# Depthwise convolution as 128x32 column blocks and a one-pass LayerNorm, in a hybrid trunk kernel

## The chip, the core and the metric

The kernel runs on one core of one Trainium2 chip. What counts is the device time of one execution in microseconds (us); the time before is the median of three runs. The profile shows one further execution, which was taken with the hardware profiler.

## The reference, cut to what matters

The program is a small diffusion backbone: four layers over 256 context and 256 latent tokens with 1024 channels, all in float32. Each layer has a token mixer and an MLP. The mixer of the second layer is a Conformer convolution, and that is where the change lies:

```python
def conformer_conv(h, w_pw1, b_pw1, w_dw, b_dw, ln_g, ln_b, w_pw2, b_pw2):
    z = h @ w_pw1 + b_pw1                      # h [B, L, 1024] -> [B, L, 2048]
    a, gt = jnp.split(z, 2, axis=-1)
    u = a * jax.nn.sigmoid(gt)
    u = lax.conv_general_dilated(u, w_dw[:, None, :], window_strides=(1,), padding=[(15, 15)],
                                 dimension_numbers=('NWC', 'WIO', 'NWC'), feature_group_count=1024) + b_dw
    u = jax.nn.silu(layer_norm(u, ln_g, ln_b))  # mean and variance over the 1024 channels of a token
    return u @ w_pw2 + b_pw2
```

The depthwise convolution gives each channel its own 31 taps along the tokens. It is run for the latent and for the context stream, separately padded.

## The kernel before, in words

All activations are kept transposed: a tile has 128 channels on the partitions and 512 tokens on the free axis (256 of the context, then 256 of the latent stream). Eight such tiles make up the 1024 channels. A float32 product is made from three matmuls at the single-pass rate: each operand is split into a high part and a rest (`hi`, `lo`), and `mm3` (L216) adds hi*hi, hi*lo and lo*hi. A weight unit of 128x1024 is loaded by a DMA into a buffer `raw` (six of them), ScalarE makes the high part `whi`, VectorE the rest `wlo` (L191; four buffers each). `project` (L222) runs the units one after the other and calls `done` on each finished PSUM bank. Dense matmuls use four PSUM banks; two banks (`w`) serve everything else in the mixer, and `nr` and `md` are single banks.

`conv(1)` (L796) has these steps. `glu(c)` (L800), for c from 0 to 7, projects the two units of channel tile c (48 matmuls of 128x512), takes the sigmoid on ScalarE and makes the tile `u` on VectorE. The depthwise convolution is shared out: tiles 0 to 2, and 3 and 4 stream by stream, are made on VectorE (`on_dve`, L826) by one multiply-add per tap; these steps stand in the list `todo`, and `taps_of` issues 12 of them per tile between the units. Tiles 5 to 7 are made on TensorE (`on_pe`, L862): for each tap GpSimd builds two 128x128 diagonal matrices (`affine_select`, L874, four taps at a time, two buffers), and three matmuls of 128x256 per tap and stream accumulate in PSUM (L882). The LayerNorm (`layer_norm`, L935) goes over one stream at a time, first the context, then the latent stream: sums over channels as matmuls with a column of ones (L943), the mean spread back over the partitions by matmuls (`spread`, L370), centring on VectorE (L957), squares on ScalarE, sums of squares, a root from Ln and Exp with a Newton step (`rsqrt`, L358), scaling (L972), SiLU and the high part on ScalarE, the rest on VectorE (L982). The second stream's tap work is woven into the first stream's LayerNorm (`norm_with`). Last, `out_project` (L432) multiplies by `conv_pw2`, adds the bias and the gated result to `x`, squares `x` for the next norm, and norms it for the MLP; its first four units run stream by stream, because of `apart`, and its last three do so too (`tail`).

The program is written with a scheduling layer that fixes the order of each engine's instructions when the kernel is built: what stands earlier in the program goes first, unless it isn't ready by the layer's own estimate of times. Semaphores and buffers follow from it. At run time each engine works through its list in order. The DMAs of weights are all issued from the SP queue, also in program order, and wait there for a free buffer.

Of the kernel before, what the change touches and what calls it, by code (L numbers as in the profile page):

```python
# [14 lines left out]
P = 128  # L15
# [28 lines left out]
PE_CONV = ((5, (0, 1)), (6, (0,)), (7, (0,)), (6, (1,)), (7, (1,)))  # L44
DVE_CONV = ((0, (0, 1)), (1, (0, 1)), (2, (0, 1)), (3, (0,)), (4, (0,)), (3, (1,)), (4, (1,)))
N_DG = 2
DG_TAPS = 4
LATE = 1
LATE_PE = 2
LN_LAG = 2  # L50
LN_ORDER = (0, 1, 2, 3, 4, 5, 6, 7)
DVE_TAPS = 12
# [22 lines left out]
CONV_ORDER = (0, 1, 2, 3, 4, 5, 6, 7)  # L75
# [3 lines left out]
def kernel(ctx: ExitStack, tc: tile.TileContext, io, out, depth=8):  # L79
# [716 lines left out]
    def conv(i):  # L796
        h = nxt.pop("h")
        cv = {}

        def glu(c):  # L800
            got = {}

            def done(n, p, zs):
                if n == 0:
                    got["a"] = p
                    taps_of(DVE_TAPS // 2)
                else:
                    sg = tmp("sg")
                    act(out=sg, in_=p, func=ACTF.Sigmoid, bias=par[:, C_BPW1 + 8 + c:C_BPW1 + 9 + c])
                    u = st("u")  # L810
                    stt(out=u, in0=got["a"], scalar=par[:, C_BPW1 + c:C_BPW1 + c + 1], in1=sg,
                        op0=ALU.add, op1=ALU.mult)
                    got["u"] = u
            project([io["conv_pw1"][c], io["conv_pw1"][8 + c]], h, (0, 1), done, first=2,
                    apart=c == CONV_ORDER[0])
            return got["u"]

        taps = [PAD] + [w for w in range(TAPS) if w != PAD]
        us = {}
# [4 lines left out]
        row = []  # L824

        def on_dve(c, zs):  # L826

            def step(n, w):
# [3 lines left out]
                if n == 0:  # L832
                    if c not in cv:
                        cv[c] = st("cv")
                    ins = ts(out=cv[c][:, span(zs)], in0=us[c][:, span(zs)], scalar1=tap, scalar2=bias_of(c),
                             op0=ALU.mult, op1=ALU.add).ins
                    if zs == (1,):
                        for name in row:
                            behind(ins, name, "the first stream first")
                else:  # L840
                    a3, u3 = [t.rearrange("p (z t) -> p z t", z=2)[:, zs[0]:zs[-1] + 1] for t in (cv[c], us[c])]
                    ins = stt(out=a3[:, :, lo:hi], in0=u3[:, :, lo + s:hi + s], scalar=tap, in1=a3[:, :, lo:hi],  # L842
                              op0=ALU.mult, op1=ALU.add).ins
                    if n == TAPS - 1 and zs != (1,):
                        row.append(ins.name)
# [15 lines left out]

        def on_pe(c, zs):  # L862

            got = {}

            def step(n, w):
                if n == 0:
                    got["u"] = ready.pop((c, zs), None) or split(c, zs)
                    got["ps"] = bank("cvps", "w")
                if n % DG_TAPS == 0:  # L870
                    k = min(DG_TAPS, TAPS - n)
                    got["dg"] = sm.tile([P, 2 * DG_TAPS, P], FR, tag="dg", name="dg", bufs=N_DG)
                    m = (pe_tiles.index(c) * TAPS + n) * 2
                    nc.gpsimd.affine_select(  # L874
                        out=got["dg"][:, 0:2 * k],
                        in_=tap_flat[:, m:m + 2 * k].unsqueeze(2).to_broadcast([P, 2 * k, P]),
                        pattern=[[0, 2 * k], [1, P]], compare_op=ALU.is_equal, fill=0.0, base=0,
                        channel_multiplier=-1)
                dg = [got["dg"][:, 2 * (n % DG_TAPS) + q] for q in range(2)]
                for q, part in ((0, 0), (0, 1), (1, 0)):  # L880
                    for z in zs:
                        mm(out=got["ps"][:, half(z)], lhsT=dg[q], rhs=got["u"][z][part][:, w:w + N_CTX],  # L882
                           start=n == 0 and q == part == 0 and z == zs[0], stop=n == TAPS - 1 and q == 1 and z == zs[-1])
                if n == TAPS - 1:
                    if c not in cv:
                        cv[c] = st("cv")
                    act(out=cv[c][:, span(zs)], in_=got["ps"][:, span(zs)], func=ACTF.Identity, bias=bias_of(c))
            return [lambda n=n, w=w: step(n, w) for n, w in enumerate(taps)]


        pe_tiles = sorted({c for c, _ in PE_CONV})
        tap_flat = cst.tile([P, len(pe_tiles) * TAPS * 2], F32, name="tap_hl")
        tap_hl = tap_flat.rearrange("p (c w q) -> p c w q", w=TAPS, q=2)
        t_ = par[:, C_TAP:C_TAP + KD * TAPS].rearrange("p (c w) -> p c w", c=KD)
        t_ = t_[:, pe_tiles[0]:pe_tiles[-1] + 1]
        for o, w in enumerate((slice(PAD, PAD + 1), slice(0, PAD), slice(PAD + 1, TAPS))):
            o = (slice(0, 1), slice(1, PAD + 1), slice(PAD + 1, TAPS))[o]
            act(out=tap_hl.bitcast(FR)[:, :, o, 0], in_=t_[:, :, w], func=ACTF.Copy)
            tt(out=tap_hl.bitcast(FR)[:, :, o, 1], in0=t_[:, :, w], in1=tap_hl[:, :, o, 0], op=ALU.subtract)
# [13 lines left out]
        ready = {}  # L913
        for n, c in enumerate(CONV_ORDER):
            us[c] = glu(c)
            for c_, zs in PE_CONV:
                if c_ == c:
                    ready[c, zs] = split(c, zs)
            for c_, zs in DVE_CONV:
                if c_ == c and zs != (1,):  # L920
                    merge(todo, on_dve(c, zs))
            if n:
# [3 lines left out]
        def both(a, b):
            while a or b:
                for q in (a, b):
                    if q:
                        q.pop(0)()  # L930

        both(todo, pe_todo)
        y = [(htile("yhi", FR), htile("ylo", FR)) for _ in range(KD)]

        def layer_norm(z):  # L935

            c_ = half(z)
            blocks = (2 * z, 2 * z + 1)
            got = {}

            def add(name, t, c):
                for n, b in enumerate(blocks):
# [448 lines left out]
```

## Time and profile before

| | us |
|---|---|
| median of three runs | 2227.54 (2226.61 to 2229.44) |
| profiled execution | 2229.72 |
| its span, first to last instruction | 2228.0 |
| TensorE busy | 2171.2 (97%) |
| VectorE busy | 1636.3 (73%) |
| ScalarE busy | 868.8 (39%) |
| GpSimd busy | 58.2 (3%) |
[...]

The profiled execution's own time is 1.7 us more than its span. Busy shares are averages over the whole program; the stage of the convolution is some 250 us of it, and its shares are read from windows of the trace. A matmul's busy time overlaps with the next one's, so the pace of matmuls is read from the distance between starts.

### The profile page before, as it was taken

Reading aid. Unit: us, or ns where it says so; the run is one execution under the profiler, and the core shown is the slowest. Engines: PE = TensorE matmul, PEld = TensorE weight load, DVE = VectorE, ACT = ScalarE, POOL = GpSimd, SP = SyncE. Lnnn points to the kernel's source line nnn. Section 1 sums busy time; section 2 is a strip of 40 time slices with the busy share of each in tenths; the row PEclk is TensorE's granted clock in tenths of the full one; section 3 lists DMA queues with packets and bytes.
Section 4 is the critical chain, followed back from the end, with each engine's and each line's share of the span. In section 5 each row is a group of like instructions: output and inputs, shape, how many; then the busy total and the mean of one; then the engine's idle time right before and its main releaser. Section 6 shows DMA issues by size and latency. Waiting matters only on the chain.

```text
span 2228.0 us, 33427 instructions
## 1 busy us (share of the span) xinstructions
PE 2171.2 (97%) x13162; PEld 1856.8 (83%) x13162; DVE 1636.3 (73%) x2989; ACT 868.8 (39%) x1495; POOL 58.2 (3%) x68
## 2 busy tenths in 40 slices
PE   6999999999999979999999998999999999999999
PEld 5777898888888979988888887788888889889999
DVE  4565577788859985777888579857788776687665
ACT  4443343233233205532322367734232324554443
POOL 0000000000000251000000000000000000000000
PEclk9999999999999979999999999999999999999999
DMA  8543334555522110345555311014455542234553
GB/s 304 173 149 133 113 103 148 184 173 198 188 98 93 39 38 10 105 149 192 170 198 181 104 67 64 14 63 146 152 192 188 177 170 86 85 114 132 186 182 117
DMA packets 83965, 299.57 MB, mean 134 GB/s; under 512 B 9440, under 2 KB 10976, under 8 KB 83808
## 3 DMA queue, kind: packets, MB, share of 16 engines
q1 hardware_dynamic: 83808, 297.44, 39.1%
q8 instruction: 103, 1.69, 0.3%
q14 instruction: 54, 0.44, 0.1%
HBM read 296.35 MB, written 1.05 MB: 133 GB/s over the span
## 4 chain that ended last, share of the span: by engine, by line
PE 88%; DVE 8%; ACT 1%; issue 1%; POOL 0%; DMA 0%; SPq 0%; POOLq 0%; DVEq 0%; ACTq 0%
PE ps L218 22%; PE ps L219 21%; PE ps L220 21%; DVE cv L842 4%; PE one L218 2%; PE one L219 2%; PE one L220 2%; PE ps L275 2%; PE ps L277 2%; PE ps L276 2%; PE o L719 1%; DVE wlo L197 1%; PE modps L292 1%; PE cvps L882 1%; PE sums L383 1%; PE sps L667 1%
## 5 line engine op out<-in xcount | busy, mean ns | idle before, releaser
L110 ACT ACTIVATE whi<-raw 128x1024 fp32r<-128x1024 f32 x366 | 387.1, 1059 | 883.2 <-PE ps L219 621.5
L197 DVE TENSOR_TENSOR wlo<-raw,whi 128x1024 fp32r<-128x1024 f32 x366 | 445.3, 1226 | 162.1 <-ACT whi L110 160.9
L218 PE MATMUL ps<-hi,whi 128*128 128x512 f32 (+1 forms) x1336 | 463.6, 348 | 0.0
L219 PE MATMUL ps<-lo,whi 128*128 128x512 f32 (+1 forms) x1336 | 461.1, 345 | 0.0
L220 PE MATMUL ps<-hi,wlo 128*128 128x512 f32 (+1 forms) x1336 | 460.9, 345 | 0.0
L218 PE MATMUL ps<-hhi,whi 128*128 128x512 f32 (+1 forms) x1240 | 437.5, 355 | 3.3 <-ACT hhi L110 3.3
L219 PE MATMUL ps<-hlo,whi 128*128 128x512 f32 (+1 forms) x1240 | 437.9, 354 | 0.0
L220 PE MATMUL ps<-hhi,wlo 128*128 128x512 f32 (+1 forms) x1240 | 436.4, 353 | 0.0
L308 DVE SCALAR_TENSOR_TENSOR macc<-modraw,cs,macc 128x512 f32<-128x512 f32 x504 | 346.9, 745 | 0.0
L218 PEld LDWEIGHTS ps<-hi,whi 128*128 128x128 f32 x1336 | 252.7, 189 | 34.0 <-issue 3.6
L220 PEld LDWEIGHTS ps<-hi,wlo 128*128 128x128 f32 x1336 | 253.0, 189 | 30.4
L219 PEld LDWEIGHTS ps<-lo,whi 128*128 128x128 f32 x1336 | 253.1, 189 | 30.1 <-issue 0.3
L218 PEld LDWEIGHTS ps<-hhi,whi 128*128 128x128 f32 x1240 | 234.3, 190 | 38.5 <-ACT hhi L110 4.0
L220 PEld LDWEIGHTS ps<-hhi,wlo 128*128 128x128 f32 x1240 | 235.1, 190 | 31.4
L219 PEld LDWEIGHTS ps<-hlo,whi 128*128 128x128 f32 x1240 | 235.4, 190 | 31.1
L449 DVE SCALAR_TENSOR_TENSOR x<-ps,mod,x 128x256 f32<-128x256 f32 x264 | 118.7, 480 | 173.6 <-PE ps L220 172.2
L842 DVE SCALAR_TENSOR_TENSOR cv<-u,par,cv 128x498 f32<-128x498 f32 (+28 forms) x210 | 128.0, 679 | 0.4
L110 ACT ACTIVATE hi<-sq 128x512 fp32r<-128x512 f32 (+1 forms) x128 | 73.7, 576 | 104.5 <-DVE sq L464 104.5
L204 DVE TENSOR_TENSOR lo<-sq,hi 128x512 fp32r<-128x512 f32 (+1 forms) x128 | 79.4, 620 | 22.1 <-ACT hi L110 22.1
L218 PE MATMUL one<-hhi,whi 128*128 128x512 f32 (+1 forms) x256 | 95.1, 372 | 0.3 <-DVE r L589 0.3
L219 PE MATMUL one<-hlo,whi 128*128 128x512 f32 (+1 forms) x256 | 91.5, 357 | 0.0
L220 PE MATMUL one<-hhi,wlo 128*128 128x512 f32 (+1 forms) x256 | 91.0, 355 | 0.0
(217 smaller groups left out, 2785.3 us busy)
## 6 DMA issues: line engine op xcount, KB each, us to landing
modraw<-in_w_mod SPq DMA_DIRECT2D x192, 512.0 KB, 3.8
raw<-in_w_mlp_in SPq DMA_DIRECT2D x128, 512.0 KB, 4.0
raw<-in_w_mlp_out SPq DMA_DIRECT2D x128, 512.0 KB, 3.3
raw<-in_conv_pw SPq DMA_DIRECT2D x24, 512.0 KB, 3.3
raw<-in_gla_v SPq DMA_DIRECT2D x16, 512.0 KB, 4.1
raw<-in_gla_r SPq DMA_DIRECT2D x16, 512.0 KB, 3.8
raw<-in_gla_out SPq DMA_DIRECT2D x16, 512.0 KB, 3.7
raw<-in_attn_qkv SPq DMA_DIRECT2D x12, 512.0 KB, 3.2
```

What stands on the lines that cost most here:

```text
L110: ins = nc.scalar.activation(**kw).ins
L197: tt(out=lo, in0=raw, in1=hi.bitcast(F32), op=ALU.subtract)
L204: tt(out=lo[:, cols], in0=src, in1=hi.bitcast(F32)[:, cols], op=ALU.subtract)
L218: mm(out=o, lhsT=wh[:, wsl], rhs=ah[:, cols], start=first, stop=False)
L219: mm(out=o, lhsT=wh[:, wsl], rhs=al[:, cols], start=False, stop=False)
L220: mm(out=o, lhsT=wl[:, wsl], rhs=ah[:, cols], start=False, stop=last)
L275: mm(out=ps[t], lhsT=ah[:, tok], rhs=wh[:, sl], start=kk == order[0] and i == 0, stop=False)
L276: mm(out=ps[t], lhsT=al[:, tok], rhs=wh[:, sl], start=False, stop=False)
L277: mm(out=ps[t], lhsT=ah[:, tok], rhs=wl[:, sl], start=False, stop=kk == order[-1] and i == 1)
L308: stt(out=acc, in0=raw[:, h], scalar=c, in1=acc, op0=ALU.mult, op1=ALU.add)
L449: stt(out=x[:, m, c], in0=src[:, c], scalar=gate[:, m, z:z + 1], in1=x[:, m, c], op0=ALU.mult, op1=ALU.add)
L842: ins = stt(out=a3[:, :, lo:hi], in0=u3[:, :, lo + s:hi + s], scalar=tap, in1=a3[:, :, lo:hi], op0=ALU.mult, op1=ALU.add).ins
```

## The change

The convolution on TensorE takes over tiles 3 to 7, and VectorE keeps tiles 0 to 2 for both streams at once. GpSimd's diagonal matrices, the split of `u`, and the work stream by stream go. Instead:

- `regroup` copies the tile `u` with sixteen VectorE copies of 32 partitions x 128 tokens into `ut`: 32 channels x 4 token phases on the partitions, and on the free axis four groups of 128 (two streams of 64 groups of four tokens).
- `on_pe` works with 34 tap matrices per tile (`BLOCKS`: shift m by groups of four tokens, output phase q). Each is a 128x128 block of which 32 columns belong to each channel group g. They are made on the host and loaded by DMA from the new array `conv_tz`, eight to a transfer of 512 KB into a `raw` buffer (five transfers per tile, the last of 128 KB). For each block and each g one float32 matmul with 32 columns and 2 x (64-|m|) tokens writes 32 partitions of the bank, every fourth token.
- `on_pe(c)` stands one tile behind `glu`: that of tile 3 after `glu(4)`, of tile 6 after `glu(7)`, and that of tile 7 inside the LayerNorm.
- 16 instead of 12 taps per tile are issued between the units.
- The LayerNorm goes over both streams at once. An early mean, from tiles 0 to 5, is taken off before the squares are made; the sums over the centred tiles and their squares give the rest of the mean and the variance; the root is a power of -0.5 on GpSimd.
- `out_project` runs its first four units together over both streams, without `apart`.

```diff
-PE_CONV = ((5, (0, 1)), (6, (0,)), (7, (0,)), (6, (1,)), (7, (1,)))
-DVE_CONV = ((0, (0, 1)), (1, (0, 1)), (2, (0, 1)), (3, (0,)), (4, (0,)), (3, (1,)), (4, (1,)))
...
-DVE_TAPS = 12
+PE_CONV = (3, 4, 5, 6, 7)
+PH = 4
+
+BLOCKS = tuple((m, q) for m in (0, -4, -3, -2, -1, 1, 2, 3, 4) for q in range(PH)
+               if any(0 <= PH * m + p - q + PAD < TAPS for p in range(PH)))
+TZ = 1024 // P
+DVE_TAPS = 16
...
+                    u = us[c] = st("u")
...
+            project([io["conv_pw1"][c], io["conv_pw1"][8 + c]], h, (0, 1), done, first=2, apart=c == 0)
...
+
+
+        def regroup(c):
+
+            ut[c] = st("ut")
+            u = us[c].rearrange("p (x j) -> p j x", j=PH)
+            for g in range(4):
+                for j in range(PH):
+                    nc.vector.tensor_copy(out=ut[c][32 * j:32 * j + 32, P * g:P * g + P],
+                                          in_=u[32 * g:32 * g + 32, j])
+
+        def on_pe(c):
+            ps = bank("cvps", "w")
+            o4 = ps.rearrange("p (z s j) -> p j z s", z=2, j=PH)
+            u4 = ut[c].rearrange("p (g z s) -> p g z s", g=4, z=2)
+            for n, (m, q) in enumerate(BLOCKS):
+                if n % TZ == 0:
+                    tz = wp.tile([P, 1024], F32, tag="raw", name="tz", bufs=N_BUF["raw"])
+                    w = P * min(TZ, len(BLOCKS) - n)
+                    nc.sync.dma_start(out=tz[:, 0:w], in_=io["conv_tz"][PE_CONV.index(c), n // TZ, :, 0:w])
+                lo, hi = max(0, -m), min(P // 2, P // 2 - m)
+                for g in range(4):
+                    r = slice(32 * g, 32 * g + 32)
+                    o = n % TZ * P + 32 * g
+                    mm(out=o4[r, q, :, lo:hi], lhsT=tz[:, o:o + 32], rhs=u4[:, g, :, lo + m:hi + m],
+                       start=n == 0, stop=n == len(BLOCKS) - 1)
+            cv[c] = st("cv")
+            act(out=cv[c], in_=ps, func=ACTF.Identity, bias=bias_of(c))
...
+        waiting = []
+        for c in range(KD):
+            glu(c)
+            if c in PE_CONV:
+                regroup(c)
+                waiting.append(c)
+                if len(waiting) > 1:
+                    on_pe(waiting.pop(0))
+            else:
+                merge(todo, on_dve(c))
+            if c:
                 taps_of(DVE_TAPS - DVE_TAPS // 2)
+        taps_of(len(todo))
+        load_table("silu_and_others")
...
+
+        blocks = (0, 1, 2, 3)
+        early = range(KD - 2)
+
+        def total(ps, t, first, last):
+            for n, b in enumerate(blocks):
+                mm(out=ps[:, n:n + 1], lhsT=t[:, b * P:b * P + P], rhs=ones, start=first and n == 0,
+                   stop=last and n == 3)
+
+        def column(name):
+            return sm.tile([P, 4], F32, tag="ln_" + name, name="ln_" + name, bufs=1)
+
+        acc = st("acc")
+        tt(out=acc, in0=cv[0], in1=cv[1], op=ALU.add)
+        for c in early[2:]:
+            tt(out=acc, in0=acc, in1=cv[c], op=ALU.add)
+        ps = bank("sums", "md")
+        total(ps, acc, True, True)
+        k_col = column("k")
+        ts(out=k_col, in0=ps[:, 0:4], scalar1=1.0 / (P * len(early)), scalar2=None, op0=ALU.mult)
+        k_row = spread(k_col, blocks)
+        sq = {}
+
+        def centre(c):
+            tt(out=cv[c], in0=cv[c], in1=k_row, op=ALU.subtract)
+            sq[c] = st("lnsq")
+            act(out=sq[c], in_=cv[c], func=ACTF.Square)
+
+        for c in early:
+            centre(c)
+        s2 = bank("lnsq", "w")
+        on_pe(waiting.pop(0))
+        for c in early:
+            total(s2, sq[c], c == 0, False)
+        s1 = bank("sums", "md")
+        for c in (KD - 2, KD - 1):
+            centre(c)
+            total(s1, cv[c], c == KD - 2, c == KD - 1)
+            total(s2, sq[c], False, c == KD - 1)
+        m, v, q, power = column("m"), column("v"), column("q"), column("power")
+        nc.vector.memset(power, -0.5)
+        ts(out=m, in0=s1[:, 0:4], scalar1=1.0 / D, scalar2=None, op0=ALU.mult)
+        m_row = spread(m, blocks, "nr")
+        tt(out=q, in0=m, in1=m, op=ALU.mult)
+        ts(out=v, in0=s2[:, 0:4], scalar1=1.0 / D, scalar2=EPS, op0=ALU.mult, op1=ALU.add)
+        tt(out=v, in0=v, in1=q, op=ALU.subtract)
+        nc.gpsimd.tensor_tensor(out=v, in0=v, in1=power, op=ALU.pow)
+        r_row = spread(v, blocks, "w")
...
+        for c in range(KD):
+            tt(out=cv[c], in0=cv[c], in1=m_row, op=ALU.subtract)
+            tt(out=cv[c], in0=cv[c], in1=r_row, op=ALU.mult)
+            act(out=cv[c], in_=cv[c], func=ACTF.Silu, scale=par[:, C_LNG + c:C_LNG + c + 1],
+                bias=par[:, C_LNB + c:C_LNB + c + 1])
+            act(out=y[c][0], in_=cv[c], func=ACTF.Copy)
+            tt(out=y[c][1], in0=cv[c], in1=y[c][0].bitcast(F32), op=ALU.subtract)
         load_table(EXP_LN)
         out_project(2 * i, [io["conv_pw2"][m] for m in range(8)], y, (0, 1), modt[i][:, 16:24],
-                    bias=par[:, C_BPW2:C_BPW2 + 8], extra=1, apart=True)
+                    bias=par[:, C_BPW2:C_BPW2 + 8], first=4)
...
+    w, r = f["conv_w_dw"][0].reshape(TAPS, KD, 4, 32), np.arange(32)
+    tz = np.zeros((len(PE_CONV), len(BLOCKS), PH, 32, 4, 32), np.float32)
+    for n, c in enumerate(PE_CONV):
+        for b, (m, q) in enumerate(BLOCKS):
+            for p in range(PH):
+                t = PH * m + p - q + PAD
+                if 0 <= t < TAPS:
+                    tz[n, b, p, r, :, r] = w[t, c].T
+    tz = tz.reshape(len(PE_CONV), len(BLOCKS), P, P)
+    tz = np.concatenate([tz, np.zeros((len(PE_CONV), -tz.shape[1] % TZ, P, P), np.float32)], axis=1)
+    a["conv_tz"] = tz.reshape(len(PE_CONV), -1, TZ, P, P).transpose(0, 1, 3, 2, 4).reshape(len(PE_CONV), -1, P, 1024)
```

## Rows read from the trace of the kernel before

**Rows 1.** Windows: stretch, its us, then busy us (instructions) per engine, clock, DMA share, GB/s.

```profile
680.40:754.20 73.80, 73.80 (x330) 61.19 (x329) 73.48 (x130) 18.47 (x25) 0.00 (x0) 1.00 0.25 86
754.20:809.20 55.00, 45.59 (x374) 44.90 (x372) 54.93 (x58) 5.10 (x8) 30.14 (x24) 0.95 0.11 33
809.20:858.10 48.90, 42.31 (x283) 41.71 (x283) 36.39 (x91) 13.57 (x30) 23.83 (x14) 0.78 0.02 8
858.10:913.40 55.30, 55.30 (x417) 54.08 (x418) 29.53 (x69) 30.58 (x58) 0.00 (x0) 0.94 0.14 48
```

**Rows 2.** Chain of work that ended last, 754 to 862 us: shares, then start, us, what.

```profile
by line: DVE cv L842 44.3%; PE cvps L882 23.1%; POOL dg L874 9.9%; PE sums L943 8.9%; DVE wlo L197 4.7%; PE lnsq L943 2.8%; issue 1.2%; PE ps L218 1.2%; PE rows L374 1.0%; PE ps L219 0.8%; PE ps L220 0.8%; DVE ulo L859 0.6%; DVE u L811 0.6%
...
757.68 40.48 DVE cv L842 x39
...
809.25 5.28 PE sums L943 x24
```

**Rows 3.** Timeline of TensorE: start, us, line, operation, tiles, shape, count.

```profile
749.65 0.39 PE L218 MATMUL ps<-hhi,whi 128*128 128x512 f32 x1
...
753.50 0.39 PE L220 MATMUL ps<-hhi,wlo 128*128 128x512 f32 x1
...
858.06 0.56 PE L218 MATMUL ps<-yhi,whi 128*128 128x256 f32 x1
...
907.75 0.28 PE L218 MATMUL ps<-yhi,whi 128*128 128x256 f32 x1
...
913.39 0.28 PE L220 MATMUL ps<-yhi,wlo 128*128 128x256 f32 x1
```

**Rows 4.** Timeline of TensorE around matmuls of 32 columns (two records each).

```profile
40.70 3.66 PE L292 MATMUL modps<-modraw,cs 128*32 128x256 f32 x64
...
661.99 0.28 PE L220 MATMUL ps<-hi,wlo 128*128 128x256 f32 x1
662.20 0.66 PE L314 MATMUL modps<-macc,pick 128*32 128x128 f32 x16
662.79 0.39 PE L218 MATMUL ps<-hhi,whi 128*128 128x256 f32 x1
```

**Rows 5.** Chain of work over the span: full-width float32 matmuls, two records each.

```profile
247.32 2.88 PE o L719 x24
...
666.40 0.79 PE sums L383 x8
```

**Rows 6.** Timeline of VectorE, 680 to 800 us.

```profile
680.41 0.74 DVE L811 SCALAR_TENSOR_TENSOR u<-ps,par,sg 128x512 f32<-128x512 f32 x1
...
682.78 6.85 DVE L842 SCALAR_TENSOR_TENSOR cv<-u,par,cv 128x482 f32<-128x482 f32 x9
...
697.45 3.33 DVE L842 SCALAR_TENSOR_TENSOR cv<-u,par,cv 128x488 f32<-128x488 f32 x5
...
734.85 1.23 DVE L197 TENSOR_TENSOR wlo<-raw,whi 128x1024 fp32r<-128x1024 f32 x1
...
774.18 23.98 DVE L842 SCALAR_TENSOR_TENSOR cv<-u,par,cv 128x492 f32<-128x492 f32 x18
```

**Rows 7.** Instructions of lines 156 and 1178: duration ns min/median/max, starts, forms.

```profile
L156 DVE CAST ident_r<-ident x1: 227/227/227, 4.3 to 4.3; 128x128 fp32r<-128x128 f32 x1
...
L1178 DVE CAST k<-kT x3: 282/283/284, 1317.2 to 1328.3; 128x128 fp32r<-128x128 f32 x3
```

**Rows 8.** Groups by line, 846 to 880 us: count, busy us, mean ns, idle before.

```profile
L972 DVE TENSOR_TENSOR cv<-cv,rows 128x256 f32<-128x256 f32 x16 | 5.7, 414 | 3.0 <-PE rows L374 3.0
...
L110 ACT ACTIVATE cv<-cv,par 128x256 f32<-128x256 f32 x16 | 9.0, 590 | 5.4 <-DVE cv L972 5.4
...
L110 ACT ACTIVATE yhi<-cv 128x256 fp32r<-128x256 f32 x16 | 6.1, 404 | 0.0
```

**Rows 9.** Groups by line of GpSimd, whole span.

```profile
L874 POOL TENSOR_SCALAR_AFFINE_SELECT dg<-tap_hl 128x768 fp32r<-128x768 f32 x5 | 5.0, 993 | 2.8 <-PE cvps L882 2.8
L856 POOL MEMSET ulo<- 128x15 f32 x12 | 0.9, 111 | 43.3 <-PE ps L219 43.2
```

**Rows 10.** The page: GB/s in 40 slices; a DMA issue with count, KB, us to landing.

```profile
GB/s 304 173 149 133 113 103 148 184 173 198 188 98 93 39 38 10 105 149 192 170 198 181 104 67 64 14 63 146 152 192 188 177 170 86 85 114 132 186 182 117
...
raw<-in_conv_pw SPq DMA_DIRECT2D x24, 512.0 KB, 3.3
```

More of the change, by code (lines that the diff above doesn't have):

```diff
@@ L832, in step @@
                 if n == 0:
[L833 to L839, printed above, removed]
-                else:
[L841 to L845, printed above, removed]
@@ L862, in on_pe @@
[L862 to L888, printed above, removed]
@@ L891, in conv @@
[L891 to L899, printed above, removed]
+                    cv[c] = st("cv")
@@ L911, in taps_of @@
             del todo[:n]
[L913 to L922, printed above, removed]
-                taps_of(DVE_TAPS - DVE_TAPS // 2)
-        pe_todo = [f for c, zs in PE_CONV if zs != (1,) for f in on_pe(c, zs)]
@@ L926, in both @@
[L926 to L932, printed above, removed]
-        y = [(htile("yhi", FR), htile("ylo", FR)) for _ in range(KD)]
[L935 to L942, printed above, removed]
-                    mm(out=got[name][:, n:n + 1], lhsT=t[:, b * P:b * P + P], rhs=ones,
-                       start=c == 0 and n == 0, stop=c == KD - 1 and n == 1)
-            def total(c):
-                if c == 0:
-                    got["sum"] = bank("sums", "w")
-                add("sum", cv[LN_ORDER[c]], c)
-            def mean():
-                m = sm.tile([P, 2], F32, tag="ln_m", name="ln_m", bufs=2)
-                ts(out=m, in0=got["sum"][:, 0:2], scalar1=1.0 / D, scalar2=None, op0=ALU.mult)
-                got["mean"] = spread(m, blocks)
-            def centre(c):
-                tt(out=cv[c][:, c_], in0=cv[c][:, c_], in1=got["mean"][:, c_], op=ALU.subtract)
-            def square_(c):
-                got[c] = tmp("lnsq")
-                act(out=got[c][:, c_], in_=cv[c][:, c_], func=ACTF.Square)
-            def total_sq(c):
-                if c == 0:
-                    got["sq"] = bank("lnsq", "w")
-                add("sq", got[c], c)
-            def root():
-                got["r"] = spread(rsqrt(got["sq"][:, 0:2], 2, 1.0 / D), blocks, "md")
-            def scale(c):
-                tt(out=cv[c][:, c_], in0=cv[c][:, c_], in1=got["r"][:, c_], op=ALU.mult)
-            def silu(c):
-                act(out=cv[c][:, c_], in_=cv[c][:, c_], func=ACTF.Silu, scale=par[:, C_LNG + c:C_LNG + c + 1],
-                    bias=par[:, C_LNB + c:C_LNB + c + 1])
-            def high(c):
-                act(out=y[c][0][:, c_], in_=cv[c][:, c_], func=ACTF.Copy)
-            def low(c):
-                tt(out=y[c][1][:, c_], in0=cv[c][:, c_], in1=y[c][0].bitcast(F32)[:, c_], op=ALU.subtract)
-            def staged(*stages):
-                steps = [[] for _ in range(KD + sum(l for l, _ in stages))]
-                o = 0
-                for lag, f in stages:
-                    o += lag
-                    for c in range(KD):
-                        steps[o + c].insert(0, (f, c))
-                return [lambda fs=fs: [f(c) for f, c in fs] for fs in steps]
-            return ([lambda c=c: total(c) for c in range(KD)] + [mean]
-                    + staged((0, centre), (1, square_), (LN_LAG, total_sq)) + [root]
-                    + staged((0, scale), (1, silu), (1, high), (1, low)))
```

50 lines of the change are left out of this document (7 added, 43 removed).

## The prediction

> **What bounds the kernel now.** I read the page first (TensorE 97% busy, so the program is a TensorE program), then the busy time of every engine in windows of the convolution stage, then the chain of waits there, then the timelines of TensorE and VectorE, and last the groups of instructions for prices. In the windows the reader is to see four stretches [rows 1]. From 680 to 754 us the `conv_pw1` projections keep TensorE full at the full clock; VectorE is as full (73.5 of 73.8 us). From 754 to 809 VectorE alone is full and TensorE has holes. From 809 to 858 the granted clock averages 0.78 and VectorE has holes too: the first stream's LayerNorm with the second stream's taps. From 858 to 913 TensorE is full with `conv_pw2`, at a mean clock of 0.94. The chain of waits [rows 2] says who ends last between 754 and 862: VectorE's taps (44%), then the tap matmuls (23%), and GpSimd's diagonals (10%). The taps there are slow ones: 18 of them take 23.98 us, 1.33 each, while GpSimd works for 30 of the 55 us; before GpSimd starts, five take 3.33, 0.67 each [rows 1, 6].
>
> So the stage stands as follows on TensorE [rows 3]. A 128x512 matmul starts every 0.2265 us ((753.50-749.65)/17), a 128x256 one every 0.12 ((913.39-907.75)/47). The projections end at 753.7, the first `conv_pw2` matmul starts at 858.1, the last ends its turn at 913.5. Between lie 104.4 us for convolution and LayerNorm, and 55.4 for `conv_pw2`. The prediction is where these two points, 858.1 and 913.5, come to lie. What follows 913.5 is the same program, so it is shifted whole.
>
> **The column blocks.** Removed are 558 matmuls of 128x256 (93 per tile and stream, for tiles 5 to 7): 67 us at 0.12, the GpSimd diagonals and the wait on them. Added are 34 blocks x 4 = 136 float32 matmuls for each of five tiles, with 32 columns and on the mean 124 tokens. Two lines of the kernel before are of this form [rows 4], two records per matmul: 64 records with 256 tokens in 3.66 us, 0.057 each, and 16 records with 128 tokens in 0.66, of which the last one's own 0.28 overlaps nothing, so 0.025 each. A full-width float32 matmul of 128 tokens takes 0.12 a record [rows 5]; so the four column groups do run beside each other. The bounds for a matmul here are 0.05 (two records at 0.025) and 0.114 (as slow as 256 tokens); with the full-width row as the far end, 0.24. I take 0.053, by the row that has the same number of tokens: 7.2 us a tile, against 15.5 and 32.6. A visit to this form costs at its two ends: the block of 16 starts 0.09 later than the matmul before would have let it, and the next starts 0.17 after its sixteen turns are over (662.79-662.62), 0.26 together. One visit per tile costs 0.3 us, one per transfer 1.3, one per block 8.8; with one per tile I take 7.5 us a tile.
>
> [...]
>
> **The loads.** Per tile come 2.2 MB of matrices, with the two weight units 3.2 MB for each step of 10.9 + 7.5 us: 175 GB/s. One slice of before moved 304, and this stretch 86, so they lie hidden [rows 1, 10]. They share the six `raw` buffers and the SP queue with the weight units, so a weight unit of the next tile queues behind a matrix that waits for its buffer. At 3.3 us from issue to landing, seven transfers strictly one after another would take 23 us instead of 18.4; that is priced with the first rival.
>
> **VectorE.** From 680.4, the first `u`, up to the last `u` it has: 11 `wlo` at 1.23 (13.5), 7 `u` at 0.74 (5.2), 93 taps, of which 12 in tile 0's own chain at 0.76 and 81 interleaved at 0.67 (63.4), and 64 regrouping copies [rows 6]. No row has a copy of 32 partitions with tokens four apart. The nearest, a 128x128 copy, is 0.227, one from PSUM 0.283 [rows 7]; below, 0.14, if each begins 0.09 before the last one ends, as the step of 0.67 within taps of 0.76 suggests. I take 0.227: 14.5. The sum is 96.6, so VectorE is free for the last `u` at 777.0. TensorE is through `glu(7)` at 753.7 + 3 x 7.5 = 776.2. That is a tie, and the order decides: in the steps of tiles 2, 3 and 4, before any column blocks, VectorE needs 16 x 0.67 + 2 x 1.23 + 0.74 = 13.9 us (17.5 with a regrouping) against TensorE's 10.9. That adds up to 12.6 us, and the four `wlo` buffers, which run one tile ahead, cover a part. The wait added is `u` and `wlo` behind taps in VectorE's list; TensorE waits for both. I take 8 us lost, between 0 and 16 (12.6 and one more regrouping, 3.6). `glu(7)` ends at 784.2, call it A.
>
> [...]
>
> **LayerNorm.** Column blocks of tiles 6 and 7 follow A: 15.0 us, and 0.9 for the second's bank, which the first must leave. The early sums, the early mean, and centring and squaring of six tiles (six of 0.74 on VectorE, of 0.62 on ScalarE) lie beside tile 7's blocks; if that cover is gone, they cost about 6. Then 24 sums of squares at 0.2 (0.79/4), 4.8, and 16 more for the last two tiles, 3.2 [rows 5]: A + 23.9. Then the tail: three small vector steps at 0.2, the power on GpSimd, which no row has (0.11 to 0.99, I take 0.5) [rows 9], four float32 matmuls of `spread` at 0.24, scaling 0.7, SiLU on 512 tokens about 0.8 (0.59 for 256), high part 0.6 [rows 8]: 4.2 us. The first `conv_pw2` matmul starts at A + 28.1 = 812.3, where before had 858.1.
>
> **`conv_pw2`.** Five units of 24 at 0.2265 and three by halves, 48 at 0.12: 44.5 us instead of 55.4, since no norm of a second stream lies among them. VectorE delivers a tile every 2.1 us (three steps of 0.7), the four units use 12 x 0.2265 = 2.7 for it, so TensorE sets the pace. I add 2 us for the clock, which at 858 was low after a thinly filled stretch (a first matmul of 0.56 instead of 0.28) [rows 3], and 2 for the buffers at the change from four units to one. It ends at 860.8 instead of 913.5: 52.7 us earlier.
>
> **The sum.** From the profiled execution's 2229.72 us (span 2228.0, 1.7 around it) that leaves 2177.0. It was 2.2 above the median of the runs, so I predict 2175.
>
> **Rivals.** First, the column blocks go at the pace of the 256-token row, 15.5 us a tile, because issue or the loads hold them: 5 x 8.0 more, less the 8 of lost order, which VectorE then no longer costs: +32, 2207. For it: the only long run of such matmuls is that row; against it: the short one is twice as fast. [...] Second, VectorE becomes the bound: copies at 0.283 (80 x 0.056 = 4.5) and 16 us of order lost instead of 8: +12.5, 2188. For it: VectorE is full already [rows 1]; against it: its slow taps go with GpSimd's work. Third, slower than before: with matrices and tokens that change at every matmul the column groups don't run beside each other, 0.24 a matmul, 32.6 us a tile: 5 x 25.1 - 8 = +117, 2292. It decides from 0.144 us a matmul, where 5 x (19.6 - 7.5) eats 52.7 + 8. Against it stand both rows of 32 columns. Fourth, the order costs nothing and the clock stays up: 2165 or a little less.
>
> **Chances.** Forecast 0.58, first rival 0.17, second 0.12, third 0.06, fourth 0.07. The range of 2156 to 2212 leaves out the third, the slower end of the first and the far end of the fourth, about 0.15. About 0.2% is what a measurement can tell from no change here. Faster by more: 0.89; within it, 0.03 (column blocks near 0.144); slower, 0.08.
>
> **What would show it.** Right: column-block records at 0.025 to 0.03, 35 to 38 us of TensorE for five tiles; taps at 0.67 throughout, GpSimd all but idle; copies at 0.23; first `conv_pw2` matmul 125 to 140 us after the first `u`, and about 48 us from there to the MLP. Wrong: records at 0.055 or more; TensorE waiting for `conv_tz` transfers; holes in TensorE ahead of a `wlo` or `u`; over 32 us from the end of `glu(7)` to `conv_pw2`; a low clock all through the LayerNorm.

## The result and the profile after

The changed kernel takes 2196.81 us (median of four runs, 2194.72 to 2199.41) against 2228.41 for the kernel before in the same session (2226.61 to 2229.44): a ratio of 0.986, 95% interval 0.9843 to 0.9877. That is 31.6 us faster. The forecast was 2175, inside a range of 2156 to 2212: the direction came as said and the column blocks cost what was forecast, but of the 53 us forecast some 21 are missing. The profiled execution took 2197.8 us (span 2196.0), and against this one the account is made. In the later sessions, in which the changed kernel was not run again, the kernel before took about 2251 us in a part of its executions and 2227 to 2231 in the others, so the experiments are read by their own medians, against the changed kernel's 2196.8, and a difference of a few us between sessions shows little.

The page's busy times, to be read beside the table of before: of GpSimd's 58.2 us 1.2 are left, VectorE lost 45, TensorE 29.

```profile
PE 2142.3 (98%) x13836; PEld 1816.5 (83%) x13836; DVE 1591.6 (72%) x2921; ACT 858.4 (39%) x1455; POOL 1.2 (0%) x5
```

The windows of the stage, with the columns of [rows 1]: projections with the blocks of tiles 3 to 5 (three rows), last column blocks, LayerNorm, `conv_pw2`.

```profile
683.00:713.00 30.00, 30.00 (x133) 24.50 (x132) 29.68 (x44) 5.28 (x7) 0.00 (x0) 1.00 0.22 71
713.00:745.00 32.00, 24.65 (x336) 18.85 (x335) 31.28 (x65) 4.19 (x5) 0.00 (x0) 0.88 0.31 103
745.00:795.00 50.00, 48.50 (x694) 41.06 (x696) 34.71 (x68) 7.27 (x9) 0.00 (x0) 0.98 0.44 147
795.00:812.00 17.00, 16.90 (x552) 15.87 (x540) 11.28 (x27) 5.05 (x7) 0.00 (x0) 1.00 0.60 200
812.00:832.00 20.00, 17.53 (x96) 17.32 (x96) 11.24 (x20) 8.10 (x13) 1.02 (x1) 0.66 0.48 182
832.00:881.00 49.00, 48.14 (x277) 42.54 (x278) 31.66 (x59) 27.85 (x46) 0.00 (x0) 0.97 0.16 55
```

Two rows stand out. In 713 to 745 TensorE is idle for 7.4 us while VectorE is full, and its clock averages 0.88. In 812 to 832 TensorE is nearly full, but at a mean clock of 0.66. Read more finely, both stretches have a part at half the clock (0.50):

```profile
718.00:722.00 4.00, 2.50 (x25) 1.32 (x28) 3.80 (x13) 0.00 (x0) 0.00 (x0) 0.50 0.02 4
...
816.00:820.00 4.00, 4.00 (x20) 4.00 (x21) 2.98 (x4) 2.42 (x4) 0.00 (x0) 0.50 0.90 343
820.00:824.00 4.00, 4.00 (x20) 4.00 (x20) 0.00 (x0) 0.00 (x0) 0.00 (x0) 0.50 0.55 207
```

The first `u` starts at 682.7 (680.4 before), the first `conv_pw2` matmul at 832.4 (858.1 before [rows 3]), the last ends at 881.1 (913.7): 32.6 us earlier, about the whole gain (the span is 32.0 us shorter).

The chain of waits through the end of the stage names the pieces (start, us, what):

```profile
776.11 7.32 PE cvps L857 x272
...
794.58 7.37 PE cvps L857 x272
801.97 6.32 DMA raw<-in_conv_pw
808.39 1.06 ACT whi L107
809.56 1.06 issue
810.62 0.69 DVE cv L914
811.34 0.64 ACT lnsq L107
812.02 5.38 PE lnsq L896 x40
817.40 1.71 PE sums L896 x8
819.11 3.41 PE lnsq L896 x16
822.52 1.71 PE sums L896 x8
824.23 1.71 PE lnsq L896 x8
825.94 3.63 PE rows L371 x16
```

A tile's 272 records of column blocks take 7.3 to 7.4 us: 0.027 a record, as forecast. Behind the blocks the sums of the LayerNorm take 13.9 us (812.0 to 825.9), where 8.0 were forecast, and the spreads (L371) 3.6.

Where TensorE waits in the projections is seen in its timeline (start, us, line, tiles, count; in brackets the idle time before and what ended it), and beside it in VectorE's:

```profile
713.53 0.39 PE L216 MATMUL ps<-hlo,whi 128*128 128x512 f32 x1
717.57 0.63 PE L857 MATMUL cvps<-ut,tz 128*32 128x128 f32 x2 [3.65 <-DVE ut L841]
718.70 0.64 PE L857 MATMUL cvps<-ut,tz 128*32 128x128 f32 x2 [0.50 <-DVE ut L841]
...
720.97 5.23 PE L857 MATMUL cvps<-ut,tz 128*32 128x128 f32 x142 [0.51 <-DVE ut L841]
726.14 0.50 PE L217 MATMUL ps<-hhi,wlo 128*128 128x512 f32 x1
```

```profile
708.02 7.18 DVE L828 SCALAR_TENSOR_TENSOR cv<-u,par,cv 128x484 f32<-128x484 f32 x11
715.12 0.74 DVE L808 SCALAR_TENSOR_TENSOR u<-ps,par,sg 128x512 f32<-128x512 f32 x1
...
716.43 4.49 DVE L841 COPY ut<-u 32x128 f32<-32x128 f32 x16
720.95 4.00 DVE L828 SCALAR_TENSOR_TENSOR cv<-u,par,cv 128x504 f32<-128x504 f32 x6
724.87 2.35 DVE L194 TENSOR_TENSOR wlo<-raw,whi 128x1024 fp32r<-128x1024 f32 x2
```

After `glu(3)` TensorE's list has two matmuls of `glu(4)` (the second is the one at 713.53) and then 148 records of column blocks of tile 3, whose tokens VectorE is only then regrouping. The third matmul of `glu(4)` comes at 726.1, when the first of its two `wlo` is ready too (724.87 plus 1.2). In VectorE's list these stand behind eleven taps, `u`, a tap, the regrouping and six taps more, although their high parts were made by 703.5. So the first tile of blocks, meant to lie behind `glu(4)`, fills a hole that the late `wlo` made, and fills it badly. The interleaved taps cost 0.65 each (7.18 for 11), as expected, and the copies 0.28 (4.49 for 16).

### The profile page after: what moved, and what is told of

Same layout as the page of the kernel before. It is cut to its first block, busy times and chain, and to the rows that moved or that the text cites. A ratio compares the mean times of both kernels' runs of the same rounds, so it can differ in the third digit from the quotient of the medians.

```text
span 2196.0 us, 34586 instructions
## 1 busy us (share of the span) xinstructions
PE 2142.3 (98%) x13836; PEld 1816.5 (83%) x13836; DVE 1591.6 (72%) x2921; ACT 858.4 (39%) x1455; POOL 1.2 (0%) x5
## 4 chain that ended last, share of the span: by engine, by line
PE 90%; DVE 6%; ACT 2%; DMA 1%; issue 1%; SPq 0%; DVEq 0%; ACTq 0%
PE ps L215 22%; PE ps L217 22%; PE ps L216 22%; PE one L215 2%; PE ps L272 2%; PE ps L274 2%; PE one L216 2%; PE ps L273 2%; PE one L217 2%; DVE cv L828 1%; PE modps L289 1%; PE o L716 1%; PE o L1160 1%; PE sums L380 1%; PE sps L664 1%; PE modps L311 1%
## 5 line engine op out<-in xcount | busy, mean ns | idle before, releaser
L201 DVE TENSOR_TENSOR lo<-sq,hi 128x512 fp32r<-128x512 f32 (+1 forms) x128 | 79.5, 621 | 22.1 <-ACT hi L107 22.1
L461 DVE TENSOR_TENSOR sq<-relu 128x512 f32<-128x512 f32 (+1 forms) x128 | 79.2, 618 | 1.9 <-ACT relu L107 1.4
```

Source lines behind the costliest of these rows:

```text
L201: tt(out=lo[:, cols], in0=src, in1=hi.bitcast(F32)[:, cols], op=ALU.subtract)
L461: tt(out=s[:, cols], in0=r[:, cols], in1=r[:, cols], op=ALU.mult)
```

## The experiments

The points by which the runs are read, all from timelines and good to about 0.1 us: the end of `glu(7)`, counted from the first `u`; the first `conv_pw2` matmul, counted from there.

| kernel | median us (range) | to the end of glu(7) | to conv_pw2 |
|---|---|---|---|
| changed | 2196.8 (2194.7–2199.4) | 111.8 | 37.9 |
| e1 regrouping on ScalarE | 2195.6 (2191.8–2196.8) | 109.0 | 40.8 |
| e2 sums with 32 columns | 2188.6 (2187.3–2191.1) | 112.3 | 31.5 |
| e3 filler matmuls | 2201.3 (2200.5–2204.0) | 111.8 | 42.4 |
| e4 old LayerNorm | 2206.1 (2202.9–2207.3) | 112.0 | 44.9 |
| e5 units ahead | 2182.3 (2180.5–2183.8) | 97.4 | 38.3 |
| e6 matrices' own queue | 2210.7 (2205.9–2211.5) | 112.9 | 47.6 |
| e7 units ahead and sums | 2174.7 (2172.7–2178.2) | 96.4 | 31.4 |
| e8 GpSimd busy | 2230.7 (2229.3–2235.1) | 146.5 | 37.6 |
| e9 twelve taps | 2187.5 (2184.5–2189.4) | 102.7 | 37.7 |
| e10 four tiles | 2176.2 (2174.3–2179.0) | 96.3 | 31.9 |
| e11 six tiles | 2182.4 (2180.5–2183.3) | 103.8 | 32.8 |
| e12 e7, regrouping on ScalarE | 2176.0 (2175.9–2177.4) | 98.5 | 31.8 |

**Are the copies the cost?**

```diff
-                    nc.vector.tensor_copy(out=ut[c][32 * j:32 * j + 32, P * g:P * g + P],
-                                          in_=u[32 * g:32 * g + 32, j])
+                    act(out=ut[c][32 * j:32 * j + 32, P * g:P * g + P], in_=u[32 * g:32 * g + 32, j],
+                        func=ACTF.Copy)
```

> The 80 regrouping copies are made by ScalarE instead of VectorE; nothing else differs from the changed kernel (2196.8 us). In its trace VectorE is full from 682.7 to 775 us and gives 22.5 us to the copies (sixteen in 4.5), TensorE waits for copies, wlo and u, and its clock falls in these waits; from the first u to the last projection it needs 14 us more than its own work. Theory: VectorE's list costs these 14 us; freed of the copies it gives back 7 to 10: 2187 to 2190 us. Rival: the matrices' loads, which hold the raw buffers, cost them (ScalarE waited 49.9 us for conv_pw loads): 2195 to 2199 us, and ScalarE's own copies then show as a new wait.

Measured: 2195.61, 1 us less. The theory's gain doesn't come, and the time is the one that the rival gave. VectorE is relieved of 80 copies and gets idle time (78.4 us busy of 108.9 up to `glu(7)`), yet the wait in front of tile 3's blocks stays, now for ScalarE's copies, of which sixteen take 7.1 us. That the loads are the reason, as the rival has it, is not shown by this run; the runs on the weight units and on the matrices' queue below speak against it.

**Are the narrow sums the loss in the LayerNorm?** The sums with a column of ones (four matmuls of one column each) become four matmuls with 32 columns of ones side by side over 128 tokens, and one small matmul turns the result.

```diff
-                mm(out=ps[:, n:n + 1], lhsT=t[:, b * P:b * P + P], rhs=ones, start=first and n == 0,
-                   stop=last and n == 3)
+                mm(out=ps[32 * n:32 * n + 32, 0:P], lhsT=ones32, rhs=t[:, b * P:b * P + P], start=first, stop=last)
```

> The LayerNorm's sums over channels use 32 columns of ones and 128 tokens in four column groups, and one further small matmul turns the four rows into columns; the rest is the changed kernel (2196.8 us). Before this edit the 80 sum records from 812 to 826 us take 13.9 us, 11 of it at half clock; the last squares are there at 818.5. Theory: the sums at that clock set the start of conv_pw2 (832.4, forecast 10 us earlier): sums ready at about 820, clock up, 2186 to 2190 us. Rival: VectorE's list (a wlo waiting for a late load ahead of the centring) sets it and the sums only fill: 2194 to 2198 us.

Measured: 2188.61, 8.2 us less, as the theory had it. Between the end of `glu(7)` and `conv_pw2` 6.4 us are saved. The windows of this kernel over the last blocks, the LayerNorm and `conv_pw2`:

```profile
795.00:814.00 19.00, 17.14 (x567) 15.71 (x562) 13.57 (x30) 6.44 (x8) 0.00 (x0) 1.00 0.68 208
814.00:826.00 12.00, 7.06 (x103) 4.13 (x95) 9.66 (x19) 6.72 (x12) 1.02 (x1) 1.00 0.75 257
826.00:875.00 49.00, 48.09 (x278) 42.63 (x279) 31.75 (x59) 27.95 (x46) 0.00 (x0) 0.97 0.17 55
```

TensorE is busy for 7.06 of 12 us in the second row and keeps the full clock (1.00), which falls only behind it, at the end of the wait of 2.85 us for the first `yhi` (0.79 from 824 to 828, 0.78 from 828 to 832); with the one-column matmuls it was busy for 17.5 of 20 and had 0.66. A busy TensorE in the profile is thus not enough to keep the clock.

**Can dense matmuls between them hold the clock?** After every four sums one matmul of 128x512 is added whose result nothing uses, eleven in all.

```diff
+            if warm:
+                mm(out=bank("warm", "pj"), lhsT=ident_r, rhs=h[0][0], start=True, stop=True)
```

> After each group of four narrow sum matmuls one idle dense matmul of 128x512 goes into a spare bank (11 of them, 2.5 us at full clock); its output is used by nothing. The rest is the changed kernel (2196.8 us). Theory: the narrow sums leave TensorE's clock low, and their pace follows the clock (0.21 us a record from 816 to 826, 0.10 at the full clock): with the fillers the clock stays up, the sums take about 10 us with the fillers instead of 13.9, the spreads and the first conv_pw2 matmuls gain 2 to 3: 2190 to 2193 us. Rival: the pace of the narrow sums doesn't follow the clock, or the clock falls all the same: the fillers come on top, 2199 us.

Measured: 2201.29, 4.5 us more; the rival holds, by its second branch: the pace follows the clock, but the clock falls all the same (1.00 from 810 to 812 us, 0.50 from 814 to 832). In TensorE's timeline the same eight records go from 0.95 us at the full clock to 1.70 at half, with the filler in between:

```profile
811.91 0.95 PE L896 MATMUL lnsq<-ones,lnsq 128*128 128x1 f32 x8
812.72 0.47 PE L899 MATMUL warm<-hhi,ident_r 128*128 128x512 f32 x1
...
815.04 1.70 PE L896 MATMUL lnsq<-ones,lnsq 128*128 128x1 f32 x8
816.60 0.77 PE L899 MATMUL warm<-hhi,ident_r 128*128 128x512 f32 x1
```

**The convolution alone.** The new convolution with the LayerNorm of before, stream by stream, and the old call of `out_project`.

```diff
+        norm_with(0)
+        load_table(EXP_LN)
+        norm_with(1)
...
+                    bias=par[:, C_BPW2:C_BPW2 + 8], extra=1, apart=True)
```

> The convolution of the changed kernel with the LayerNorm and conv_pw2 of the kernel before (stream by stream, mean before squares, root by Ln and Exp, halves in conv_pw2), started once tile 7's blocks are issued. Theory: the gain of 31.6 us comes from the convolution (its blocks, and VectorE's taps without GpSimd beside them); the new norm starts conv_pw2 no earlier than the old one's first stream would, and saves only conv_pw2's halves: 2201 to 2206 us. Rival: the one-pass norm is the larger part: 2212 us or more.

Measured: 2206.13, at the edge of what the theory gave. Of the 31.6 us the convolution brings 22 and the one-pass LayerNorm with the joint `conv_pw2` 9. How much of the 22 comes from the column blocks and how much from VectorE's faster taps is not separated.

**VectorE's order or the loads?** `project` takes units that were made earlier, and `glu(c)` makes those of `glu(c + 1)` ahead of its taps.

```diff
                     got["a"] = p
+                    if c < KD - 1:
+                        ahead[c + 1] = [unit(io["conv_pw1"][m]) for m in (c + 1, 9 + c)]
                     taps_of(DVE_TAPS // 2)
```

> The two weight units of the next tile are issued when the first bank of a tile is done, ahead of that step's taps, instead of behind them; TensorE's list then has tile 3's column blocks behind glu(4) and not behind glu(3). Theory (the 13.8 us that the projections lose come from VectorE's list: wlo of the next tile behind taps and regrouping, so that TensorE takes up blocks whose tokens aren't regrouped yet): glu(7) ends some 100 to 104 us after the first u instead of 111.8, taps stay at 0.65, total 8 to 11 us below the changed kernel's 2196.8: 2186 to 2189. Rival one (the matrices' transfers hold SP's queue and the raw buffers): 2194 to 2199. Rival two (VectorE is full anyway, so the wait only moves): u of the last tile as late as before, 2194 to 2199.

Measured: 2182.34, 14.5 us less, more than the theory's 8 to 11. The stretch up to `glu(7)` shrinks by 14.4 us; the one behind it stays (38.3 for 37.9). Its windows over the projections:

```profile
681.00:713.00 32.00, 32.00 (x143) 26.48 (x142) 31.68 (x46) 7.81 (x10) 0.00 (x0) 1.00 0.30 98
713.00:745.00 32.00, 31.00 (x506) 26.68 (x508) 31.43 (x65) 4.08 (x5) 0.00 (x0) 1.00 0.28 106
745.00:778.00 33.00, 33.00 (x504) 28.24 (x495) 31.38 (x66) 4.08 (x5) 0.00 (x0) 1.00 0.53 189
```

TensorE's 7.4 us of idle time between 713 and 745 have become 1.0, and the clock stays at 1.00. Over the whole stretch, from the first `u` to the end of `glu(7)`, TensorE is idle for 1.0 us instead of 8.9 and busy for 96.4 instead of 102.9, at a mean clock of 1.00 instead of 0.95: some 8 of the 14.4 us were waiting and 6.5 were matmuls drawn out by the low clock. VectorE does the same work (94.8 us busy, 95.9 in the changed kernel), with 2.6 us of idle time instead of 15.8.

The other explanation is that the matrices' transfers block the weights. In the changed kernel ScalarE waits 49.9 us in seven pieces for `raw<-in_conv_pw`. So the matrices get three buffers of their own and GpSimd's queue (two of the 45 buffers for activations, `st`, give the room):

```diff
-                    tz = wp.tile([P, 1024], F32, tag="raw", name="tz", bufs=N_BUF["raw"])
+                    tz = wp.tile([P, 1024], F32, tag="tz", name="tz", bufs=3)
...
-                    nc.sync.dma_start(out=tz[:, 0:w], in_=io["conv_tz"][PE_CONV.index(c), n // TZ, :, 0:w])
+                    nc.gpsimd.dma_start(out=tz[:, 0:w], in_=io["conv_tz"][PE_CONV.index(c), n // TZ, :, 0:w])
```

> The matrices get three buffers of their own and GpSimd's DMA queue; the weights keep the six raw buffers and SP's queue to themselves. Rival one of the run before: ScalarE's waits for raw<-in_conv_pw (49.9 us in seven) go, and 5 to 10 us with them: 2187 to 2192. Theory: TensorE's list still has tile 3's blocks in front of glu(4), so the wait for the regrouped tokens (some 6.5 us and the clock with it) stays and at most 1 to 3 us are gained: 2193 to 2197.

Measured: 2210.66, 13.9 us more, which neither expectation had. Waits of this kernel, 690 to 850 us (who waited for whom: us in total, times, longest):

```profile
ACT whi L107 <- PE ps L216: 50.9, 6, 11.3
...
PE cvps L857 <- DMA tz<-in_conv_tz: 6.4, 4, 2.4
```

ScalarE's waits for loads are gone; it waits as long for TensorE to free `whi` buffers. Up to `glu(7)` nothing is gained (112.9), so there those 49.9 us cost nothing. Instead TensorE waits for matrices, and the blocks of tiles 6 and 7 with the early sums take 24.8 us (798.6 to 823.4) instead of 17.5. Six shared buffers were the better arrangement; whether it is the three buffers, GpSimd's queue or the two `st` buffers fewer that cost here was not taken apart.

**Do the two losses add?** The edits of e2 and e5 together.

```diff
+                        ahead[c + 1] = [unit(io["conv_pw1"][m]) for m in (c + 1, 9 + c)]
...
+                mm(out=ps[32 * n:32 * n + 32, 0:P], lhsT=ones32, rhs=t[:, b * P:b * P + P], start=first, stop=last)
```

> The first of these runs and the sums with 32 columns (8.2 us by themselves) together. Theory: the two losses lie in different stretches and add, 17 to 19 us below the changed kernel: 2178 to 2181, near the forecast of 2175. Rival (one loss in two guises: VectorE is late for both): no better than the sums alone, 2186 to 2190.

Measured: 2174.70, 22.1 us less, more than the theory's 17 to 19, which had counted on 8 to 11 us for the order; 8.2 and the measured 14.5 would be 22.7, so they add. This is the fastest version, and its time is what was forecast for the change. That is partly luck: up to `glu(7)` it needs 7.4 us less than forecast (96.4 for 103.8), and from there to `conv_pw2` 3.3 more (31.4 for 28.1). Its windows, with the projections, the last blocks, the LayerNorm (with the wait before `conv_pw2`) and `conv_pw2`:

```profile
713.00:745.00 32.00, 32.00 (x539) 27.70 (x541) 31.42 (x66) 4.07 (x5) 0.00 (x0) 1.00 0.30 111
745.00:777.00 32.00, 32.00 (x472) 27.36 (x460) 31.30 (x65) 4.07 (x5) 0.00 (x0) 1.00 0.52 194
777.00:796.00 19.00, 17.23 (x562) 15.78 (x564) 13.67 (x32) 7.12 (x9) 0.00 (x0) 1.00 0.68 213
796.00:809.00 13.00, 7.07 (x114) 4.74 (x104) 10.66 (x21) 7.24 (x12) 1.02 (x1) 0.94 0.64 231
809.00:858.00 49.00, 48.54 (x275) 42.76 (x275) 30.69 (x57) 27.12 (x44) 0.00 (x0) 0.95 0.17 55
```

**What idle GpSimd was worth.** Selects like those that built the diagonals are put back, for nothing: `diagonals(c, 8)` makes eight of 128x1024, which read `us[c]`.

```diff
+            if 0 < c < 6:
+                diagonals(c, 8)
             if c in PE_CONV:
                 regroup(c)
```

> GpSimd makes eight selects of 128x1024 for each of tiles 1 to 5 (some 40 us in all), which nothing uses; all else as in the changed kernel. Theory (GpSimd's work, not the number of streams or the form, made a tap cost 1.33 us in the kernel before): taps that run beside a select take about 1.3 us again instead of 0.65, VectorE needs up to 20 us more before the last u, total 10 to 20 us longer: 2207 to 2217. Rival (taps were slow for another reason): taps at 0.65, 2195 to 2199.

Measured: 2230.71, 33.9 us more, beyond the theory's 10 to 20, and the time is about that of the kernel before. VectorE's timeline in this kernel, and GpSimd's:

```profile
693.95 14.96 DVE L828 SCALAR_TENSOR_TENSOR cv<-u,par,cv 128x502 f32<-128x502 f32 x14
...
728.08 10.88 DVE L848 COPY ut<-u 32x128 f32<-32x128 f32 x16
...
745.17 9.91 DVE L828 SCALAR_TENSOR_TENSOR cv<-u,par,cv 128x498 f32<-128x498 f32 x15
```

```profile
692.23 11.60 POOL L838 TENSOR_SCALAR_AFFINE_SELECT dg<-u 128x1024 fp32r<-128x1024 f32 x8 [691.74 <-DVE u L808]
709.72 12.07 POOL L838 TENSOR_SCALAR_AFFINE_SELECT dg<-u 128x1024 fp32r<-128x1024 f32 x8 [5.88 <-DVE u L808]
727.63 9.23 POOL L838 TENSOR_SCALAR_AFFINE_SELECT dg<-u 128x1024 fp32r<-128x1024 f32 x8 [5.84 <-DVE u L808]
```

With GpSimd idle (from 745) fifteen taps take 9.91, 0.66 each. Fourteen taps of which the first ten or so us lie beside a select take 14.96, 1.07 on the mean; the two from 711.37, wholly beside a select, take 3.02, where the same two in the changed kernel took 1.37 (705.61). Sixteen copies take 10.88 instead of 4.49, 0.68 each on the mean; the five from 757.07, wholly beside a select, take 5.50, 1.10 each. Up to `glu(7)` the taps cost VectorE 10.8 us more (71.3 for 60.5), as the theory had it, and the copies, which it left out, 19.0 more (36.5 for 17.5). So the 33.9 us are not what the change gained by an idle GpSimd: the kernel before had no such copies. Why taps and copies are slower beside a select, no run shows.

**Fewer taps a step.** The same order of TensorE's list by another way.

```diff
-DVE_TAPS = 16
+DVE_TAPS = 12
```

> Twelve taps instead of sixteen between the units of a tile, all else as in the changed kernel; TensorE's list then has the same order as in the run with the weight units ahead. Theory (the loss in the projections is wlo behind too many taps): glu(7) ends 98 to 102 us after the first u, as it did there (97.4), and the nine taps that are left over (6 us) lie beside the blocks of tiles 5 to 7: 2182 to 2187. Rival (it was the early issue of the loads that helped): 2192 to 2199.

Measured: 2187.46, 9.3 us less, half a microsecond past the theory's end; `glu(7)` ends after 102.7 us, also just past it, for 3.0 us of waiting for a `wlo` remain. As expected, TensorE's list has all 272 records of tile 3 behind `glu(4)` (722.7 to 730.0). The rival is out: no weight unit stands earlier in the program here, and most of the gain is there.

**Which engine is the bound then?** Four tiles and six on TensorE, and the copies on ScalarE, all with the edits of e7. The run with four tiles has the copies on ScalarE too, by the edit that stands last here.

```diff
-PE_CONV = (3, 4, 5, 6, 7)
+PE_CONV = (4, 5, 6, 7)
...
-DVE_TAPS = 16
+DVE_TAPS = 18
```

> Weight units ahead, sums with 32 columns, regrouping on ScalarE, and TensorE takes four tiles (4 to 7) instead of five; VectorE has 124 taps, 18 a step. Theory (with the order mended TensorE is the bound up to glu(7), a tile of blocks costs it 7.4 us): 5 to 8 us below the 2174.7 of units ahead with the sums: 2167 to 2170. Rival (VectorE, with 20 us of taps more and 23 us of copies fewer, ends no sooner, and its last taps hold the early mean): 2174 to 2182.

Measured: 2176.21; the theory is wrong here and the rival right. The stretch to `glu(7)` is 96.3 us, as with five tiles: VectorE is now full without a gap (95.65 of 96 us), and TensorE waits. The sum of its windows from 682 to 778 us (us of the stretch, busy us of each engine, means over three windows):

```profile
sum 96.00, PE 92.26 PEld 75.77 DVE 95.65 ACT 36.24 POOL 0.00; mean PE 30.75 PEld 25.26 DVE 31.88 ACT 12.08 POOL 0.00
```

```diff
-PE_CONV = (3, 4, 5, 6, 7)
+PE_CONV = (2, 3, 4, 5, 6, 7)
```

> Weight units ahead, sums with 32 columns, six tiles (2 to 7) on TensorE. Theory (TensorE is the bound, 7.4 us a tile): 6 to 8 us above 2174.7: 2181 to 2183. Rival (VectorE is still the bound, and is relieved of 31 taps for 16 copies, 15.6 us): 2165 to 2174.

Measured: 2182.38, 7.7 us more than e7: one tile of blocks, which is 7.4 in the trace. The theory holds. VectorE is busy for 79 of 103 us, TensorE for all (windows from 681 to 784):

```profile
sum 103.00, PE 103.00 PEld 88.41 DVE 79.28 ACT 16.50 POOL 0.00; mean PE 34.33 PEld 29.47 DVE 26.43 ACT 5.50 POOL 0.00
```

```diff
-                    nc.vector.tensor_copy(out=ut[c][32 * j:32 * j + 32, P * g:P * g + P],
+                    act(out=ut[c][32 * j:32 * j + 32, P * g:P * g + P], in_=u[32 * g:32 * g + 32, j],
```

> Weight units ahead, sums with 32 columns, regrouping on ScalarE, five tiles. Theory (TensorE is the bound up to glu(7), and VectorE's copies lie beside it): within 2 us of 2174.7. Rival (VectorE is the bound): 4 to 8 us below it.

Measured: 2176.04, within 2 us of e7, as the theory had it. Five tiles are the balance of the two engines: a tile more costs TensorE 7.4 us, and one fewer fills VectorE.

## Why the prediction was right, and where it was off

By the profiled executions 2177.0 was forecast and 2197.8 measured, 20.8 us more. The median lies inside the range, but nearer to the second rival (2188) and the first (2207) than to the forecast; which terms came is read from the trace:

- **Column blocks: right.** 0.027 a record (272 records in 7.32 us, chain, 776.11) and 7.4 us a tile against 7.2 to 7.5. The first rival (15.5) and the third (32.6) are out.
- **Taps: right.** 0.67 was taken, 0.65 measured, and e8 shows that taps beside GpSimd's selects are slow (two in 3.02 us instead of 1.37), as those of before were (18 in 23.98 [rows 6]).
- **Copies: price too low, with little effect.** 0.28 from start to start instead of 0.227, 3.4 us for 64 of them. A copy lasts 0.27 (median of the 80), so on the mean one begins only when the last one is over, while taps that last 0.73 follow each other at 0.65; why copies don't overlap, no run shows. Taken off VectorE, all 80 change the total by 1.2 us (e1) and 1.3 the other way (e12), so they lie mostly beside other work.
- **Order in the projections: the place right, the size too small.** Allowed were 8 us, within 0 to 16, for `u` and `wlo` behind taps in VectorE's list. e5 takes this loss away and it is 14.4 us; the rest of the stretch is 97.4 where 95.8 was forecast. Together `glu(7)` ended 8.0 us later after the first `u` (111.8 for 103.8). What the term lacked is the second step: the scheduling layer, which fixes the lists at build time, filled the hole with blocks whose tokens weren't regrouped, so that TensorE waited for copies one by one and its clock fell to half (0.50 from 718 to 722).
- **LayerNorm: 9.8 us late.** The sums were priced at 0.2 a matmul from a row at the full clock [rows 5], 8.0 us; 13.9 were measured, since the clock fell during them: eight records take 0.81 us from start to start at the full clock (e3, 811.91 to 812.72), which would be 8.1 for 80, and 1.71 at half (chain, 817.40 to 819.11). The tail was 6.5 instead of 4.2: the spreads ran mostly at half clock (0.50 from 824 to 828; 3.63 for 16 records) and the power on GpSimd took 1.02. And the sums began 1.6 later, because centring stands behind a `wlo` whose weights had come late (chain, 801.97 to 810.62); the prediction took the loads as hidden. These are 5.9, 2.3 and 1.6. e2 gives back 6.4 of the 9.8 in this stretch. "A low clock all through the LayerNorm" stood among the signs of a wrong prediction, but had no term of the sum nor a rival of its own.
- **`conv_pw2`: right.** 48.7 us from the first matmul to the end of the last, against 48.5.
- **The start:** the first `u` is 2.3 us later than before, in e5 0.3; in the experiments it lies between 680.2 (e3) and 685.7 (e6). This is in front of the changed code, and its cause is open.

8.0, 9.8, 0.2 and 2.3 make 20.3 of the 20.8 us. The second rival (VectorE as the bound, 2188) had the sizes nearly right, copies at 0.283 (0.28 measured) and 16 us for the order (14.4). With them `glu(7)` would have ended 116.3 us after the first `u`; 111.8 were measured. Its title is wrong all the same: VectorE's sum fits into 97.4 us (e5), its order didn't. Of the signs of a wrong prediction three came: holes in TensorE ahead of a `wlo` (and of regrouped tokens), more than 32 us from `glu(7)` to `conv_pw2` (37.9), and the low clock. So the total lies inside the range only because the range was wide: the two terms that were too small together cost 17.8 us.

## What to carry to other kernels

When work moves to an engine that has room by its sum, look at the order of the lists as well: preparing the next tile's weights ahead of a long run of interruptible work was worth 14.5 us here, without a single instruction less. Sums over partitions with a column of ones let TensorE's clock fall here (0.50 from 816 to 824 us); as 32 columns side by side they kept it at full (1.00 from 814 to 826 in e2), which was worth 8.2 us. And idle GpSimd was worth something to VectorE here (e8: two taps in 1.37 us instead of 3.02, a copy in 0.28 instead of 1.10): a change that removes its selects should be credited with faster taps and copies beside them.

## What the runs showed of the hardware

TensorE's granted clock fell from full (1.00) to half (0.50) while it was busy throughout with one-column float32 matmuls (816 to 824 us), and one dense 128x512 matmul after every eight records did not keep it up (0.50 from 814 to 832 us, e3); with 32-column sums it stayed at 1.00 although TensorE was idle for 5 of 12 us (e2). In four 32-column groups a float32 matmul of 124 tokens on the mean started every 0.054 us over a whole tile (272 records in 7.32 us). Beside GpSimd's selects five 32x128 copies on VectorE took 5.50 us, 1.10 each instead of 0.28, two taps 3.02 instead of 1.37, and a `wlo` of 128x1024 2.10 instead of 1.22 (e8).
